# A fused transformer block on one core: column sums issued later, and a block compression with both halves of its weights side by side

## The chip, the cores and the metric

One core of a Trainium2 chip. The time is device microseconds of one execution of the program; the median of several runs is given. Engines are named as in the profile: PE (TensorE: matmuls; PEld its weight loads), DVE (VectorE), ACT (ScalarE), POOL (GpSimd), SP (SyncE, which here only issues DMAs).

## What is computed

Two transformer blocks in a row on 512 tokens of width 1024 in float32. The first block is attention of two kinds with a mixture of experts; the change doesn't touch it. The second has two layers, each a mixer and an MLP of width 4096:

```python
for layer in range(2):
    h = rms_norm(x, norm_mix_pre[layer])
    m = mixer_a(h, ...) if layer == 0 else mixer_c(h, ...)
    x = x + rms_norm(m, norm_mix_post[layer])
    h = rms_norm(x, norm_mlp_pre[layer])
    x = x + rms_norm(relu(h @ w1) ** 2 @ w2, norm_mlp_post[layer])
```

`mixer_c` compresses its keys and its values before it attends to them. From each of 31 windows of 32 tokens, which start 16 tokens apart, it makes one vector per group, for four groups of width 64:

```python
idx = 16 * arange(31)[:, None] + arange(32)[None, :]
def compress(z, pe, w1, w2):                  # w1: (32, 64, 64)
    blk = z[:, idx] + pe[:, None, :]
    hdn = gelu(einsum('bnlgd,lde->bnge', blk, w1))
    return hdn @ w2
```

## The kernel before

Activations lie transposed: 128 of the 1024 features on the partitions, tokens along the free dimension. Weights come by DMA on SP's queue as slabs of 128 x 1024 floats, and each is split into a high part (ACT, line 167) and a low part (DVE, line 168). A product is then three matmuls per block of 128 features: high by high (line 195), low by high (198), high by low (199). One such triple is called a step below; with 256 tokens a pass over 8 output chunks of 8 blocks is 64 steps.

The end of each mixer and of each MLP runs in halves of 256 tokens (`halves`). A first pass does chunk 0 for both halves and the other seven for the first half. A second pass does seven chunks, 56 steps, for the second half. While PE runs the second pass, the first half is finished by `post`, a Python generator that `weave` advances by one `yield` for each step of the pass. `post` for the second half is handed on and is woven into the opening pass of whatever follows, one `yield` for two steps: the first 64 steps of the MLP, or the opening of `mixer_c` (32 steps of chunks, then the values, where two steps count as one).

`post` does this: column sums of the squares of the mixer's output (`rstd`, with `col_sum` at line 325, a power on POOL, and `spread` matmuls), one `yield`; then for each of 8 blocks of features the normed output (DVE, line 1509), the new `x` (POOL, 1510), its high and low part for what follows (ACT 364, DVE 365), its square (ACT 281, the last one 290) and the running sum `acc` (DVE, 282), one `yield` each; then some empty yields; then `col_mean` of the new `x`, which is eight small matmuls with one moving column (line 325) and one DVE operation. `mlp_left` keeps the result in `mlp_eps`, which is read at the end of the MLP. `mix_left` makes `mix_rcol` (POOL, 1542) and `mix_rrow` (PE, 1547; ACT, 1549) of it, which the evacuations of `mixer_c` read. The empty yields are 12 ahead of an MLP and 4 ahead of `mixer_c`.

The order in the text is not the order on the engines. A planner deals the instructions out to the engines before the run: of those that it reckons ready at a time it takes the one that comes first in the text. What stands in an engine's queue is then fixed and runs in that order.

`compress` runs twice, for values and for keys. It loads its weights into a free part of `x` as 16 blocks of 128 x 64, each for two neighbouring tokens (`z` holds a copy of itself on partitions 64 to 127, one token further on). 16 products with 31 columns per group (line 1986) add up the 32 tokens of a window, 16 more with one column (line 1990) make the bias from `pe`. Each is two PE instructions in the trace. Then follow the bias (DVE), a gelu (DVE and ACT), and a product with `w2` (lines 2005 and 2014). Between its parts, `yield 1`, `yield 6` and `yield 3` let as many steps of the gates and projections through.

Of the kernel before, what the change touches and what calls it, by code (L numbers as in the profile page):

```python
# [9 lines left out]
F32 = mybir.dt.float32  # L10
# [4 lines left out]
OP = mybir.AluOpType  # L15
# [4 lines left out]
P = 128  # L20
S = 512
# [37 lines left out]
R1 = 0.4  # L59
R5 = 0.4  # L60
APP = 0

def run(steps):
    for _ in steps:
        pass


def weave(main, *fill):  # L70

    fill = chain(*fill)
    due = 0.0
    for n in main:
        due += n
        while due >= 1:
            next(fill, None)
            due -= 1
    run(fill)


class Net:
# [284 lines left out]
    def apply(self, x, g, r, hi, lo, bias=None):  # L367
# [5 lines left out]
        t = self.np.tile([P, 256], F32, name="ap_t", bufs=APB)  # L373
        if bias is None and APP:
            nc.gpsimd.tensor_mul(t, x, r)
# [1119 lines left out]
            self.nc.scalar.dma_start(x[:, k:k + 4], xr[:, k:k + 4])  # L1495
        return x

    def post(self, acc, g, tok, nxt, dump, save=False, left=None, eps=None):


        nc, m = self.nc, self.m
        r = self.rstd(acc, D, eps=eps)
        yield 1
        x = self.x
        acc = self.acc_tile("acc2")
        o = self.t["out"].rearrange("(k p) t -> p k t", p=P)
        for k in range(NC):
            t = self.np.tile([P, 256], F32, name="ap_t", bufs=APB)
            nc.vector.scalar_tensor_tensor(t, m[:, k, tok], g[:, k:k + 1], r, op0=OP.mult, op1=OP.mult)  # L1509
            nc.gpsimd.tensor_add(x[:, k, tok], x[:, k, tok], t)  # L1510
            if left is not None:
                self.raw_apply(x[:, k, tok], nxt[:, k:k + 1], self.h[0][:, k, tok], self.h[1][:, k, tok])
            if nxt is not None:
                self.sq_half(acc, x[:, k, tok], k, nc.vector if k >= PSQ else nc.gpsimd)
            elif k % 2:
                nc.sync.dma_start(o[:, k - 1:k + 1, tok], x[:, k - 1:k + 1, tok])
            yield 1
        self.dump(dump, x[:, :, tok], (slice(None), slice(None), tok))
        if nxt is not None:
            if save:  # L1520
                self.save_x(x, tok)
            if left is not None:
                for _ in range(12 if left == self.mlp_left else 4):
                    yield 1
                yield from left(self.col_mean(acc, D), tok)
                return
            r = self.rstd(acc, D)
            yield 1
            yield from self.apply_steps(x, nxt, r, tok)
# [22 lines left out]
    def halves(self, src, s0, rhs, g, nxt, dump, evac, save=False, left=None, eps=(None, None)):  # L1552

        accs, seen = [self.acc_tile("acc") for _ in range(2)], [0, 0]

        def e(i, ps, hb):
            tok = self.HALVES[hb]
            evac(i, ps, tok)
            self.sq_half(accs[hb], self.m[:, i, tok], seen[hb])
            seen[hb] += 1  # L1560

        out = [self.half_steps(src, s0, o, lambda hb: tuple(a[:, :, self.HALVES[hb]] for a in rhs), e, pool)
               for o, pool in zip(self.orders(NC, BOTH), ((), PL2))]
        tails = [self.post(accs[hb], g, tok, nxt, dump, save, left, eps[hb]) for hb, tok in enumerate(self.HALVES)]
        run(out[0])
        weave((RATE for _ in out[1]), tails[0])
        return tails[1]
# [407 lines left out]
    def compress(self, nm, z, tp, Kc, Vc):  # L1975
        nc, t = self.nc, self.t
        w1 = self.x[:, 4:6] if nm == "k" else self.x[:, 6:8]
        w1 = w1.rearrange("p k t -> p (k t)").rearrange("p (a e) -> p a e", a=16)
        w2 = tp.tile([64, 64], F32, name="cw2")
        nc.sync.dma_start(w1, t[f"cmp_w1_{nm}"].rearrange("(a p) e -> p a e", p=P))  # L1980
        nc.sync.dma_start(w2, t[f"cmp_w2_{nm}"])
        nc.gpsimd.memset(z[64:P, :, S - 1:], 0.0)
        ps = self.ptile()
        hv = ps[:64, :124].rearrange("p (g n) -> p g n", g=4)
        for a in range(16):
            nc.tensor.matmul(hv, w1[:, a], z[:, :, 2 * a:2 * a + 481:16], start=(a == 0), stop=(a == 15))
        pb = self.ptile()
        pe = self.v(f"pe_{nm}")
        for a in range(16):
            nc.tensor.matmul(pb[:64, :1], w1[:, a], pe[:, a:a + 1], start=(a == 0), stop=(a == 15))  # L1990
        yield 1
        bias = tp.tile([64, 1], F32, name="c_b")
        nc.vector.tensor_copy(bias, pb[:64, :1])
        x, u = tp.tile([64, 124], F32, name="c_x"), tp.tile([64, 124], F32, name="c_u")
        nc.vector.tensor_scalar(x, ps[:64, :124], bias, None, op0=OP.add)
        nc.vector.tensor_mul(u, x, x)
        nc.vector.tensor_scalar(u, u, 0.044715, 1.0, op0=OP.mult, op1=OP.add)
        nc.vector.tensor_mul(u, u, x)
        nc.scalar.activation(u, u, AF.Tanh, scale=0.7978845608028654)
        nc.vector.scalar_tensor_tensor(u, u, 1.0, x, op0=OP.add, op1=OP.mult)  # L2000
        nc.vector.tensor_scalar(u, u, 0.5, None, op0=OP.mult)
        yield 6
        ps = self.ptile()
        if nm == "k":
            nc.tensor.matmul(ps[:64, :124], w2, u, start=True, stop=True)
            src = ps[:64, :124].rearrange("p (g n) -> p g n", g=4)
            c = slice(32, 63)
            nc.scalar.copy(Kc["k1"][:64, :, c], src)
            nc.vector.tensor_sub(Kc["k2"][:64, :, c], src, Kc["k1"][:64, :, c])
            for d in (Kc["k1"][64:], Kc["k3"][:64]):  # L2010
                nc.vector.tensor_copy(d[:, :, c], Kc["k1"][:64, :, c])
        else:
            for g in range(4):
                nc.tensor.matmul(ps[:31, 64 * g:64 * g + 64], u[:, 31 * g:31 * g + 31], w2, start=True, stop=True)
            src = ps[:31, :256].rearrange("p (g d) -> p g d", g=4)
            for r in range(4):
                c = slice(64 * (r % 2), 64 * (r % 2) + 64)
                nc.scalar.copy(Vc[0][32 * r:32 * r + 31, :, c], src)
                if r < 2:
                    nc.vector.tensor_sub(Vc[1][32 * r:32 * r + 31, :, c], src, Vc[0][32 * r:32 * r + 31, :, c])  # L2020
        yield 3
# [264 lines left out]
```

## Time and profile before

| | |
|---|---|
| median of 3 runs | 2320.84 us (2317.47 to 2324.62) |
| the profiled execution | 2322.31 us |
| its span, first to last instruction | 2320.6 us |
| mean granted TensorE clock | 0.969 |
| PE busy | 2191.8 us (94%) |
| PEld busy | 1828.6 us (79%) |
| DVE busy | 1392.3 us (60%) |
| ACT busy | 1110.4 us (48%) |
| POOL busy | 419.1 us (18%) |

All from one profiled execution, but for the first row. A busy PE is not a PE at its peak, since its matmuls overlap and its clock has two levels; how fast it goes is read from the distance of the starts of like matmuls. A granted clock of 1.00 is 2.4 GHz, 0.50 is 1.2 GHz.

### The profile page before, as it was taken

The page shows a single profiled execution, that of the slowest core. Times are in us where ns is not written, and L with a number is a line of the kernel's source. Part 1 is how long each engine was busy: PE and PEld are TensorE (multiplying, and loading weights), DVE is VectorE, ACT ScalarE, POOL GpSimd, SP SyncE. Part 2 cuts the span into 40 slices and gives each one's busy share as a digit, 9 for nine tenths or more (in the row PEclk, how much of TensorE's full clock was granted, in tenths as well). Part 3 has the DMA queues.
Part 4 walks back from the last instruction along what each step waited for, and adds up shares of the span by engine and source line. Part 5 has one row for each costly group of instructions (what it writes and reads, how often), then busy time and mean ns, then how long its engine had stood idle before and what let it go on. Part 6 is the DMA issues. An engine that isn't in the chain of part 4 may idle for free. (4 is left out here: it accounts for less than half of the span.)

```text
span 2320.6 us, 32117 instructions
## 1 busy us (share of the span) xinstructions
PE 2191.8 (94%) x12260; PEld 1828.6 (79%) x12260; DVE 1392.3 (60%) x1994; ACT 1110.4 (48%) x1854; POOL 419.1 (18%) x470
## 2 busy tenths in 40 slices
PE   5999999979999999999899999999999998999996
PEld 4778778967888797678898888987666688888886
DVE  7676765569999856664533344564777745343443
ACT  3554542448888764445543223352565635432231
POOL 4101000221111151101300000350234332000004
PEclk9999999979999989999899999999999998999998
DMA  6563264469999631124132222342122141322221
GB/s 238 148 190 109 82 218 164 174 231 357 356 354 354 226 140 49 63 72 169 65 118 92 100 100 92 100 132 59 45 69 61 44 154 61 126 96 100 96 77 37
DMA packets 127124, 320.10 MB, mean 138 GB/s; under 512 B 24720, under 2 KB 30096, under 8 KB 126963
## 3 DMA queue, kind: packets, MB, share of 16 engines
q1 hardware_dynamic: 111902, 286.56, 35.3%
q0 software_dynamic: 11200, 22.91, 4.1%
q10 hardware_dynamic: 3860, 8.51, 1.0%
q8 instruction: 98, 1.61, 0.3%
q14 instruction: 64, 0.52, 0.1%
HBM read 296.31 MB, written 18.69 MB: 136 GB/s over the span
## 5 line engine op out<-in xcount | busy, mean ns | idle before, releaser
L195 PE MATMUL acc<-h_hi,w_hi 128*128 128x512 f32 (+1 forms) x1464 | 520.1, 356 | 3.7 <-DVE q L428 1.7
L199 PE MATMUL acc<-h_hi,w_lo 128*128 128x512 f32 (+1 forms) x1464 | 513.5, 351 | 1.3 <-DVE w_lo L168 1.2
L198 PE MATMUL acc<-h_lo,w_hi 128*128 128x512 f32 (+1 forms) x1464 | 513.2, 351 | 0.0
L168 DVE TENSOR_TENSOR w_lo<-x_raw,w_hi 128x1024 fp32r<-128x1024 f32 x260 | 317.9, 1231 | 208.0 <-ACT w_hi L167 203.7
L167 ACT CAST w_hi<-x_raw 128x1024 fp32r<-128x1024 f32 x260 | 271.2, 1047 | 290.8 <-PE acc L198 246.0
L195 PEld LDWEIGHTS acc<-h_hi,w_hi 128*128 128x128 f32 x1464 | 284.1, 194 | 37.0 <-issue 2.7
L199 PEld LDWEIGHTS acc<-h_hi,w_lo 128*128 128x128 f32 x1464 | 283.6, 194 | 36.0 <-DVE w_lo L168 2.8
L198 PEld LDWEIGHTS acc<-h_lo,w_hi 128*128 128x128 f32 x1464 | 283.9, 194 | 29.9 <-issue 0.8
L168 DVE TENSOR_TENSOR w_lo<-w_raw,w_hi 128x1024 fp32r<-128x1024 f32 (+2 forms) x141 | 166.8, 1184 | 149.0 <-ACT w_hi L167 145.0
L167 ACT CAST w_hi<-w_raw 128x1024 fp32r<-128x1024 f32 (+2 forms) x141 | 143.6, 1019 | 223.9 <-PE acc L198 197.9
L195 PE MATMUL acc<-act_hi,w_hi 128*128 128x512 f32 (+1 forms) x640 | 222.7, 348 | 0.0
L198 PE MATMUL acc<-act_lo,w_hi 128*128 128x512 f32 (+1 forms) x640 | 222.5, 348 | 0.0
L199 PE MATMUL acc<-act_hi,w_lo 128*128 128x512 f32 (+1 forms) x640 | 222.4, 348 | 0.0
L282 POOL TENSOR_TENSOR acc<-acc,sq 128x256 f32<-128x256 f32 x60 | 54.7, 911 | 744.4 <-ACT sq L281 743.4
L195 PEld LDWEIGHTS acc<-act_hi,w_hi 128*128 128x128 f32 x640 | 121.7, 190 | 15.3 <-ACT act_hi L1610 0.3
L199 PEld LDWEIGHTS acc<-act_hi,w_lo 128*128 128x128 f32 x640 | 121.7, 190 | 15.0
L198 PEld LDWEIGHTS acc<-act_lo,w_hi 128*128 128x128 f32 x640 | 121.6, 190 | 15.0
L505 DVE TENSOR_TENSOR pl<-pexp,ph 128x512 fp32r<-128x512 f32 x144 | 116.9, 824 | 24.8 <-ACT ph L504 23.0
L1615 DVE TENSOR_TENSOR m<-m,acc 128x512 f32<-128x512 f32 (+1 forms) x64 | 35.2, 552 | 137.1 <-PE acc L199 137.1
L469 DVE TENSOR_REDUCE mx<-acc 128x1 f32<-128x128 f32 x192 | 89.0, 484 | 38.8 <-PE acc L468 37.1
L503 ACT ACTIVATE pexp<-sT 128x512 f32<-128x512 f32 x144 | 82.3, 572 | 32.6 <-PE sT L494 14.0
L195 PE MATMUL gu<-w_hi,xh 128*128 128x512 f32 x240 | 95.3, 397 | 0.0
(587 smaller groups left out, 4452.8 us busy)
## 6 DMA issues: line engine op xcount, KB each, us to landing
x_raw<-mlp_w SPq DMA_DIRECT2D x90, 512.0 KB
w_raw<-mlp_w SPq DMA_DIRECT2D x48, 512.0 KB
x_raw<-w_down SPq DMA_DIRECT2D x40, 512.0 KB
x_raw<-w_up SPq DMA_DIRECT2D x39, 512.0 KB
x_raw<-w_gate SPq DMA_DIRECT2D x38, 512.0 KB
w_raw<-w_in SPq DMA_DIRECT2D x20, 512.0 KB
h_raw<-w_up SPq DMA_DIRECT2D x19, 512.0 KB
h_raw<-w_gate SPq DMA_DIRECT2D x18, 512.0 KB
```

What stands on the lines that cost most here:

```text
L167: nc.scalar.copy(hi[:, :n], raw[:, :n])
L168: (eng or nc.vector).tensor_sub(lo[:, :n], raw[:, :n], hi[:, :n])
L195: mm(ps, l[0], r[0], start=start, stop=False)
L198: mm(ps, l[0], r[1], start=False, stop=False)
L199: return mm(ps, l[1], r[0], start=False, stop=stop).ins
L282: (eng or nc.gpsimd).tensor_add(acc[:, a:a + 256], acc[:, a:a + 256], sq)
L469: self.last_max = nc.vector.reduce_max(mx[:, c0 + qb:c0 + qb + 1], ps[:, :n], axis=AX.X).ins
L503: nc.scalar.activation(e[:, :o], ps[:, :o], AF.Exp)
L505: nc.vector.tensor_sub(pt[1][:, :o], e[:, :o], pt[0][:, :o])
L1615: nc.vector.tensor_add(self.m[:, i, tok], self.m[:, i, tok], ps)
```

## The change

The empty yields become a table. Ahead of an MLP they are 40 for the first half and 22 for the second, where both were 12; ahead of `mixer_c` they are 34 and 10, where both were 4. The last MLP has no `col_mean` and so none.

In `compress` the 32 tokens of a window are taken as two halves of 16. The weights of both halves lie side by side as 8 blocks of 128 x 128, loaded by two DMAs instead of one. 8 products with 32 blocks of 16 tokens per group give the first half's part on partitions 0 to 63 and the second's on 64 to 127; 8 more with two columns of `pe` give the bias in two parts, into the same PSUM tile. ACT copies the second half's part to partitions 0 to 63, DVE adds the bias parts, and one DVE operation adds the first half's part of block n, the bias, and the second half's part of block n + 1. The clearing of the last column of `z` on POOL goes.

```diff
--- before.py
+++ after.py
@@ -59,6 +59,7 @@
 R1 = 0.4
 R5 = 0.4
 APP = 0
+LATE = ((40, 22), (34, 10))
 
 
 
@@ -1495,7 +1496,8 @@
             self.nc.scalar.dma_start(x[:, k:k + 4], xr[:, k:k + 4])
         return x
 
-    def post(self, acc, g, tok, nxt, dump, save=False, left=None, eps=None):
+    def post(self, acc, g, tok, nxt, dump, save=False, left=None, eps=None, late=0):
+
 
 
         nc, m = self.nc, self.m
@@ -1520,7 +1522,7 @@
             if save:
                 self.save_x(x, tok)
             if left is not None:
-                for _ in range(12 if left == self.mlp_left else 4):
+                for _ in range(late):
                     yield 1
                 yield from left(self.col_mean(acc, D), tok)
                 return
@@ -1561,7 +1563,8 @@
 
         out = [self.half_steps(src, s0, o, lambda hb: tuple(a[:, :, self.HALVES[hb]] for a in rhs), e, pool)
                for o, pool in zip(self.orders(NC, BOTH), ((), PL2))]
-        tails = [self.post(accs[hb], g, tok, nxt, dump, save, left, eps[hb]) for hb, tok in enumerate(self.HALVES)]
+        tails = [self.post(accs[hb], g, tok, nxt, dump, save, left, eps[hb], LATE[save][hb])
+                 for hb, tok in enumerate(self.HALVES)]
         run(out[0])
         weave((RATE for _ in out[1]), tails[0])
         return tails[1]
@@ -1975,24 +1978,28 @@
     def compress(self, nm, z, tp, Kc, Vc):
         nc, t = self.nc, self.t
         w1 = self.x[:, 4:6] if nm == "k" else self.x[:, 6:8]
-        w1 = w1.rearrange("p k t -> p (k t)").rearrange("p (a e) -> p a e", a=16)
+        w1 = w1.rearrange("p k t -> p (k t)").rearrange("p (a h e) -> p a h e", a=8, h=2)
         w2 = tp.tile([64, 64], F32, name="cw2")
-        nc.sync.dma_start(w1, t[f"cmp_w1_{nm}"].rearrange("(a p) e -> p a e", p=P))
+        src = t[f"cmp_w1_{nm}"].rearrange("(h a p) e -> h p a e", p=P, h=2)
+        for h in range(2):
+            nc.sync.dma_start(w1[:, :, h], src[h])
         nc.sync.dma_start(w2, t[f"cmp_w2_{nm}"])
-        nc.gpsimd.memset(z[64:P, :, S - 1:], 0.0)
+
         ps = self.ptile()
-        hv = ps[:64, :124].rearrange("p (g n) -> p g n", g=4)
-        for a in range(16):
-            nc.tensor.matmul(hv, w1[:, a], z[:, :, 2 * a:2 * a + 481:16], start=(a == 0), stop=(a == 15))
-        pb = self.ptile()
+        hv = ps[:, :P].rearrange("p (g n) -> p g n", g=4)
+        w1 = w1.rearrange("p a h e -> p a (h e)")
         pe = self.v(f"pe_{nm}")
-        for a in range(16):
-            nc.tensor.matmul(pb[:64, :1], w1[:, a], pe[:, a:a + 1], start=(a == 0), stop=(a == 15))
+        for a in range(8):
+            nc.tensor.matmul(hv, w1[:, a], z[:, :, 2 * a:2 * a + 497:16], start=(a == 0), stop=(a == 7))
+        for a in range(8):
+            nc.tensor.matmul(ps[:, P:P + 2], w1[:, a], pe[:, a:a + 9:8], start=(a == 0), stop=(a == 7))
         yield 1
-        bias = tp.tile([64, 1], F32, name="c_b")
-        nc.vector.tensor_copy(bias, pb[:64, :1])
-        x, u = tp.tile([64, 124], F32, name="c_x"), tp.tile([64, 124], F32, name="c_u")
-        nc.vector.tensor_scalar(x, ps[:64, :124], bias, None, op0=OP.add)
+        bias, h2 = tp.tile([64, 1], F32, name="c_b"), tp.tile([64, P + 2], F32, name="c_u")
+        nc.scalar.copy(h2, ps[64:P, :P + 2])
+        nc.vector.tensor_add(bias, ps[:64, P:P + 1], h2[:, P + 1:])
+        x, u = tp.tile([64, 124], F32, name="c_x"), h2[:, :124]
+        nc.vector.scalar_tensor_tensor(x.rearrange("p (g n) -> p g n", g=4), hv[:64, :, :31], bias,
+                                       h2[:, :P].rearrange("p (g n) -> p g n", g=4)[:, :, 1:], op0=OP.add, op1=OP.add)
         nc.vector.tensor_mul(u, x, x)
         nc.vector.tensor_scalar(u, u, 0.044715, 1.0, op0=OP.mult, op1=OP.add)
         nc.vector.tensor_mul(u, u, x)
```

## Rows read from the trace of the kernel before

**Rows 1.** The page, part 1: busy us, share of the span, instructions.

```profile
PE 2191.8 (94%) x12260; PEld 1828.6 (79%) x12260; DVE 1392.3 (60%) x1994; ACT 1110.4 (48%) x1854; POOL 419.1 (18%) x470
```

**Rows 2.** Waits of PE: who <- whom, us in total, times, longest.

```profile
PE csum L325 <- DVE acc L282: 22.5, 6, 4.5
```

**Rows 3.** PE's timeline at four waits: start, us; in brackets the idle time.

```profile
1116.21 0.24 PE L325 MATMUL csum<-ones,acc 128*128 128x1 f32 x1 [4.50 <-DVE acc L282]
...
1151.18 0.34 PE L325 MATMUL csum<-ones,acc 128*128 128x1 f32 x1 [3.60 <-DVE acc L282]
...
1494.13 0.34 PE L325 MATMUL csum<-ones,acc 128*128 128x1 f32 x1 [3.89 <-DVE acc L282]
...
1526.48 0.34 PE L325 MATMUL csum<-ones,acc 128*128 128x1 f32 x1 [2.41 <-DVE acc L282]
```

**Rows 4.** Line 195 (one a step) from pass start to wait; PE count first.

```profile
1097.90:1111.70 13.80, 9.21 (x32) 6.03 (x32) 1.00 0.11 38
1128.75:1147.50 18.75, 13.39 (x48) 8.99 (x47) 1.00 0.48 170
1473.15:1490.20 17.05, 11.94 (x42) 7.86 (x41) 1.00 0.19 63
1503.15:1524.00 20.85, 13.46 (x47) 8.76 (x46) 1.00 0.22 77
```

**Rows 5.** PE's timeline, like matmuls ahead of the first wait and behind it.

```profile
1110.83 0.28 PE L195 MATMUL acc<-h_hi,w_hi 128*128 128x256 f32 x1
1110.95 0.28 PE L198 MATMUL acc<-h_lo,w_hi 128*128 128x256 f32 x1
...
1119.44 0.41 PE L195 MATMUL acc<-h_hi,w_hi 128*128 128x256 f32 x1
1119.65 0.41 PE L198 MATMUL acc<-h_lo,w_hi 128*128 128x256 f32 x1
```

**Rows 6.** Stretches behind waits: us, busy PE, PEld, DVE, ACT, POOL; granted clock.

```profile
1116.83:1123.66 6.83, 6.83 (x34) 6.83 (x33) 0.32 (x2) 1.42 (x4) 2.00 (x3) 0.50 0.01 2
...
1150.96:1161.20 10.24, 10.02 (x47) 10.05 (x48) 2.70 (x9) 3.33 (x9) 1.18 (x1) 0.50 0.01 2
...
1492.30:1499.12 6.82, 4.99 (x23) 4.95 (x24) 3.70 (x7) 3.30 (x9) 3.34 (x5) 0.50 0.79 246
...
1918.96:1925.79 6.83, 5.37 (x25) 5.40 (x26) 2.03 (x6) 2.53 (x7) 2.88 (x4) 0.50 0.00 0
...
1956.51:1963.33 6.82, 6.54 (x31) 6.25 (x30) 1.29 (x5) 2.56 (x7) 0.00 (x0) 0.50 0.00 0
```

**Rows 7.** ACT's timeline: the last square of x in the second wait.

```profile
1153.30 0.40 ACT L290 ACTIVATE sq<-x 128x256 f32<-128x256 f32 x1
```

**Rows 8.** The stretch ahead of the second wait, columns as in rows 6.

```profile
1128.75:1147.50 18.75, 18.75 (x156) 18.40 (x154) 14.61 (x24) 12.37 (x29) 6.60 (x7) 1.00 0.48 170
```

**Rows 9.** PE's timeline, the first compression and its product with w2.

```profile
1558.53 6.94 PE L1986 MATMUL acc<-m,x 128*64 128x124 f32 x32
1565.29 1.99 PE L1990 MATMUL acc<-vec,x 128*64 128x1 f32 x32
1567.21 0.54 PE L195 MATMUL acc<-h_hi,w_hi 128*48 128x512 f32 x1
...
1573.74 0.63 PE L2014 MATMUL acc<-cw,c_u 64*31 64x64 f32 x8
```

**Rows 10.** Column sums without a wait: us, busy PE and PEld, clock.

```profile
1099.10:1099.75 0.65, 0.65 (x6) 0.65 (x6) 1.00 0.00 0
```

**Rows 11.** DVE's timeline, the end of the first gelu.

```profile
1569.40 0.22 DVE L2001 TENSOR_SCALAR c_u<-c_u 64x124 f32<-64x124 f32 x1
```

**Rows 12.** Waits of SP, 1500 to 1600 us: us in total, times, longest.

```profile
SPq L1981 <- PE acc L2014: 21.7, 1, 21.7
```

**Rows 13.** 1600 to 1880 us: PE's waits; DMA issues, median us to landing.

```profile
PE acc L467 <- DMA q<-q: 3.1, 3, 1.9
...
q<-q POOLq DMA_DIRECT2D x7, 256.0 KB, 5.2
```

## Prediction

> **What bounds the kernel now.** The page comes first: TensorE is busy 2191.8 of 2320.6 us, so in most stretches the time is the length of PE's own queue, and time can only be won where PE stands idle, runs at its lower clock, or does work that can be left out [rows 1]. The view of who waited for whom, for PE alone, is read next. Its largest entry is a wait of a column sum (`csum`, line 325) for the running sum of squares (`acc`, line 282): 22.5 us in 6 waits, the longest 4.5 [rows 2]. The timeline shows where they are: 4.50 us at 1116.21 and 3.60 at 1151.18 (the first `out_proj` and the first MLP's opening pass), 3.89 at 1494.13 and 2.41 at 1526.48 (end of that MLP, start of `mixer_c`) [rows 3]. The other two, in the second `out_proj` and the second MLP, are what is left: 22.5 - 4.50 - 3.60 - 3.89 - 2.41 = 8.1 us. PE takes its queue in order, so every one of these waits holds back matmuls whose operands are ready.
>
> Then the same stretches with the granted clock. Behind each wait PE runs at the lower of its two levels (0.50, which is 1.2 of 2.4 GHz): it is busy 6.83 us in 1116.83 to 1123.66, 10.02 us in 1150.96 to 1161.20, 5.37 and 6.54 us behind the two waits of the second `out_proj`, and 4.99 us behind the wait at 1494 [rows 6]. What that costs is read from the distance between starts of 256-column matmuls: 1110.83 to 1110.95, 0.12 us, at full clock; 1119.44 to 1119.65, 0.21 us, at the low one [rows 5]. Of a low-clock stretch 1 - 0.12/0.21 = 0.43 is lost.
>
> **The column sums, place by place.** `post` is a side thread that is advanced one `yield` at a time while a pass of matmuls runs. The change only adds empty yields ahead of `col_mean`. Where that puts the eight column-sum matmuls I count in steps of the pass (one step is three matmuls, 3 x 0.12 = 0.36 us). In the first `out_proj` the old text puts them behind 1 + 8 + 12 = 21 yields, so into step 22; in the trace 32 steps ran between the start of that pass and the stall [rows 4]. So the planner that orders the engines held them back by ten steps on its own reckoning of when `acc` is ready, and was still 4.50 us, 12.5 steps, too early. A new place counts only if it is later than the one the planner chose: new place = the later of text and planner.
>
> First half of each `out_proj`: the new text is 1 + 8 + 40 = 49 yields, step 50 of 56. PE is needed to be past step 32 + 12.5 = 44.5 for the sum to be ready. 50 is behind that by 5.5 steps, 2.0 us, so the 4.50 us go. Second half (the MLP's opening pass, one yield in two steps): old text step 44, found at 48 by the count that includes both edges [rows 4]; needed 3.60 / 0.36 = 10 steps more, 58. New text 2 x 32 = step 64, the last of the pass. The last square (ACT) starts at 1153.30 and takes 0.40 [rows 7]; PE, which stopped near 1147.58 (1151.18 - 3.60), would get to step 64 some 16 to 17 steps later, at 1153.4 to 1153.7. I take this as no wait, with 0.5 us as its upper bound. The second layer has the same structure. Idle time won: 4.50 + 3.60 + 8.1 = 16.2 us.
>
> With the waits the low clock behind them should go, as no other stop of that size stands in front of these four stretches: (6.83 + 10.02 + 5.37 + 6.54) x 0.43 = 28.8 x 0.43 = 12.4 us. The lower bound is 0, if the clock falls there anyway. (The Trainium skill, TensorE: Matmul & The Clock Gate, Terms, prices a throttled time at 1 - K/N, here one half, so 14.4 us for the same time; the rows give 0.43, since the full-clock distance of 0.12 us is not half of 0.21. The row is used.)
>
> In `mixer_c` the story differs. First half: old text step 14, found at step 42 [rows 4]; needed 3.89 / 0.36 = 10.8 more, about 53. The new text is 1 + 8 + 34 = 43 yields, step 44. That is later than the planner's 42 by only two steps. Second half: old text step 28, found after 47 k-steps [rows 4]; the new text is step 40, which is 48 k-steps (32 of the chunks, then two to a step). So one. I book 2 x 0.36 + 0.36 = 1.1 us and let the rest of these waits stand. Upper bound: both waits and the low clock of 1492.30 to 1499.12 go, 3.89 + 2.41 + 4.99 x 0.43 = 8.4 us. Lower bound: 0. I take 1.1, since the counts are rows and a later reckoning by the planner is not.
>
> What moves with the sums: behind them come a 128x2 operation on DVE (nobody waits for `mlp_eps` until the MLP's end) and, in `mixer_c`, the power on POOL, the `spread` matmuls and `mix_rrow`; POOL has `nsa_setup` queued behind the power. They move by the same one to two steps, under 1 us, which I book at nothing: until then PE has matmuls of the pass in its queue, and where the pass runs out the next one follows; without that cover it would be their length, under 1 us in each half.
>
> **What is late next.** With PE no longer stopped, ACT and DVE must deliver the split weights at the full rate. In the stretch ahead of the second stall, PE is busy 18.75 of 18.75 us, DVE 14.61 and ACT 12.37 [rows 8], with the split in it; both have room. I book nothing, and up to 2 us in each of four places for the range.
>
> **The compression.** Now: 32 matmul instructions of 124 columns from 1558.53 to 1565.29, 6.76 us, 0.211 each, then 32 of one column to 1567.21, 1.92 us [rows 9]. That is 8.7 us per pass, PE without a gap. After: 16 of 128 columns and 16 of two, with 128 weight columns instead of 64. The moving operand keeps its step of 16 tokens, so I scale by columns: 0.211 x 128/124 = 0.218, 16 x 0.218 = 3.49 us. The bias matmuls are too short to be set by two columns; the nearest row is the column sum, one column against 128 weight columns: six in 0.65 us, 0.108 each [rows 10], so 16 x 0.108 = 1.73 us. Halving their number therefore wins almost nothing. New pass 5.2, won 3.5, in two passes 6.9 us. All of it is PE time with PE busy on both sides, so it counts in full.
>
> The lower bound for this term: if the wider weight load doesn't hide under the matmul, 16 x 0.108 = 1.7 us more per pass, 3.5 in all, leaving 3.4. (The Trainium skill, TensorE: Matmul & The Clock Gate, Part 3, The mechanism, says that a weight load overlaps running matmuls only if its row group differs, which it doesn't here; by that the sum would be 3.5 us smaller. The trace speaks against it: 256-column matmuls with 128 weight columns start every 0.12 us [rows 5], while a load of that width alone takes 0.108 [rows 10].)
>
> Behind the matmuls the chain gets one ACT copy out of PSUM and one small DVE addition longer, and loses a copy. It ended at 1569.40 + 0.22 = 1569.62; PE came for it at 1573.74 [rows 9, 11]. Those 4.1 us are steps of the gate projection, which stay; the two operations cost well under 1 us, so nothing. If that cover were gone, their length would be PE's wait, twice. The two cleared columns on POOL go: nobody waited. On SP each 512 KB weight load becomes two of half the size, one issue more each; SP waited 21.7 us behind `cw2` for the first compression to end [rows 12], with PE not starved, so a second issue costs nothing there.
>
> **Sum.** 16.2 + 12.4 + 1.1 + 6.9 = 36.6 us. The profiled execution took 2322.31 us around its span of 2320.6, and the runs' median is 2320.84, so the profile is 1.5 us above the median. From the median: 2284 us.
>
> **Rivals.** (a) The planner puts the `mixer_c` sums late enough too, because its reckoning shifts with the rest: 8.4 instead of 1.1, 2277 us. Against it: the counts above. (b) The idle time goes and the clock falls nonetheless, or ACT and DVE fall behind by a similar amount: 12.4 us come back, 2297 us. For it: in the stall at 1151 the tail's last additions were DVE's, which has little left over in such a pass; against it: no stop of PE is left ahead of those stretches. (c) The change doesn't do what it says: the planner keeps the sums about where they are, since the text was not what set their place; only the compression counts, 2314 us. Against it: a planner can't easily put an instruction ahead of matmuls that the text has earlier and that are ready. (d) Slower: the order of all engines from 1558 on is dealt anew, and the DMA copies of q (POOL queue, 256 KB, 5.2 us to landing) come onto PE's path in each of the eight head pairs, where now PE waits 3.1 us for them in three waits [rows 13]. Eight waits of 5.2 us, each with the low clock that followed a wait of 4.50 (6.83 x 0.43 = 2.9), less the 3.1: 62 us, so 2346. It decides from 36.6 / 8 = 4.6 us a pair. Against it: the compression's instructions stand before all pairs and only get shorter.
>
> **Chances.** Forecast 0.55, (a) 0.13, (b) 0.20, (c) 0.08, (d) 0.04. Range 2270 to 2303: it takes in (a), the forecast and (b), with 6 to 7 us on either side for the bounds of the compression (3.5) and of the split weights; left out are (c) and (d), and the far ends. A measurement of this kernel can tell about 0.3%, 7 us: faster means under 2314, which (c) just misses or meets. Faster 0.92, same 0.06, slower 0.02.
>
> **What would show it.** In the profile after, PE's waits for `acc` of line 282 should have four entries fewer and two of about 3 and 2 us left, near the start of `mixer_c`. The low clock behind 1116, 1151, 1919 and 1957 should be gone: a low clock there without a wait says (b). The compression should show 16 matmuls of 128 columns at 0.218 us and 16 short ones at 0.108; 0.33 for the former says that loads aren't hidden. If column sums sit at their old step counts, it is (c). Waits for copies of q beyond 10 us say (d). The forecast is wrong if the second halves' sums, now last in their pass, wait for the final square by more than 0.5 us each.

## The result and the profile after

The changed kernel takes 2288.77 us (median of four runs, 2284.09 to 2293.03) where the kernel before takes 2322.73 beside it: 34.0 us less, ratio 0.9854 with an interval of 0.9822 to 0.9885. The forecast was 2284, 36.6 us less, and a range of 2270 to 2303. The profiled execution after has a span of 2291.3 us, 29.3 under that of before. Timed a second time, in the run `after_again` below, the ratio was 0.9872 (0.9850 to 0.9894).

The page's line of busy times, part 1, answers to [rows 1]: PE has 64 instructions and 16.0 us of work less, and idles 13.3 us less.

```profile
PE 2175.8 (95%) x12196; PEld 1816.5 (79%) x12196; DVE 1388.9 (61%) x1994; ACT 1109.7 (48%) x1856; POOL 422.4 (18%) x468
```

The waits of PE, the view of [rows 2] and [rows 13] (who waited for whom: us in total, times, longest). Lines of the code have moved down by one, so line 325 of before is 326 here, and 282 is 283.

```profile
PE csum L326 <- DVE acc L283: 5.1, 2, 3.1
...
PE acc L468 <- DMA q<-q: 2.5, 3, 1.6
...
PE csum L326 <- POOL acc L283: 1.2, 2, 0.6
...
PE spread L1549 <- POOL mix_rcol L1544: 0.7, 1, 0.7
```

The first entry was 22.5 us in 6. Four waits are gone and two are left, of the size that was booked. The third and the fourth are new and small: the next column sum in the same pass, that of the other half, waits for POOL once in each layer, and the spread of `mixer_c` waits for the power on POOL once. The copies of q cost 2.5 us where they cost 3.1.

PE's timeline at the places of [rows 3] (start, us; idle time in brackets): the first two rows are the first `out_proj`, then the MLP's opening pass, `mixer_c` twice, and the second layer's two.

```profile
1119.96 0.28 PE L326 MATMUL csum<-ones,acc 128*128 128x1 f32 x2
1124.48 0.38 PE L326 MATMUL csum<-ones,acc 128*128 128x1 f32 x2 [0.61 <-POOL acc L283]
...
1148.56 0.28 PE L326 MATMUL csum<-ones,acc 128*128 128x1 f32 x2
...
1480.86 0.35 PE L326 MATMUL csum<-ones,acc 128*128 128x1 f32 x2 [3.08 <-DVE acc L283]
...
1514.79 0.35 PE L326 MATMUL csum<-ones,acc 128*128 128x1 f32 x2 [2.05 <-DVE acc L283]
...
1906.55 0.28 PE L326 MATMUL csum<-ones,acc 128*128 128x1 f32 x2
...
1935.20 0.28 PE L326 MATMUL csum<-ones,acc 128*128 128x1 f32 x2
```

The same stretches by window (us, then busy time of PE, PEld, DVE, ACT and POOL, granted clock, DMA share, GB/s), against [rows 6] and [rows 8]:

```profile
1097.00:1127.00 30.00, 28.93 (x241) 28.51 (x240) 16.07 (x29) 16.02 (x37) 13.60 (x16) 1.00 0.06 20
1127.00:1150.00 23.00, 23.00 (x193) 22.77 (x192) 18.46 (x33) 16.88 (x42) 9.24 (x9) 1.00 0.41 137
1481.31:1491.55 10.24, 9.58 (x45) 9.28 (x45) 1.75 (x4) 2.04 (x5) 5.39 (x6) 0.50 0.52 170
1515.45:1522.27 6.82, 6.82 (x35) 6.82 (x34) 4.08 (x8) 3.56 (x8) 2.93 (x8) 0.50 0.94 290
1900.00:1935.00 35.00, 34.37 (x285) 33.91 (x285) 24.83 (x44) 23.68 (x56) 16.37 (x18) 1.00 0.27 91
```

At `out_proj` and the MLP the clock is 1.00 throughout, and PE is busy 23.00 of 23.00 us with DVE at 18.46 and ACT at 16.88: neither is late. In `mixer_c`, behind the two waits that were left, the low clock lasts 10.24 and 6.83 us; before it lasted 6.82 us behind the first [rows 6] and 3.41 behind the second (from 1526.42).

The compression, PE's timeline, against [rows 9]: 16 instructions of 128 columns from 1547.93 to 1551.40, 0.217 each, then 16 of two columns to the next matmul at 1553.24, 0.115 each. That is 5.3 us where 8.7 were.

```profile
1547.93 3.65 PE L1993 MATMUL acc<-m,x 128*128 128x128 f32 x16
1551.40 1.98 PE L1995 MATMUL acc<-vec,x 128*128 128x2 f32 x16
1553.24 0.64 PE L196 MATMUL acc<-h_hi,w_hi 128*48 128x512 f32 x1
```

**Where the time went, stretch by stretch.** The DVE operation that writes `w_lo` runs 464 times, in the same order in every kernel here. The start of one such operation, less the start of the same one in the profile of before, says how far a kernel is ahead at that point; the difference between two points is what it won (negative) in the stretch between them. The seven points stand at 1075, 1170, 1492, 1554, 1599, 1888 and 1972 us of the profile of before. "Sums 1" is the first `out_proj` with the MLP's opening pass, "sums 2" the second layer's. The stretch from 1170 to 1492 is left out: it moved by 0.04 us at most in every kernel; so is the tail behind 1972.

| kernel | to 1075, untouched | sums 1 | mixer_c | compression | pairs, untouched | sums 2 |
|---|---|---|---|---|---|---|
| before_again | +0.92 | -2.31 | -0.58 | +0.06 | +0.50 | -0.17 |
| the changed kernel | +1.93 | -15.23 | +2.75 | -7.26 | +2.08 | -13.49 |
| after_again | +2.22 | -15.22 | -1.40 | -7.25 | +2.12 | -13.50 |
| late_only | -1.28 | -15.21 | +1.37 | +0.03 | +3.79 | -13.49 |
| cmp_only | -1.61 | -1.98 | -1.02 | -7.24 | -1.69 | +2.19 |
| mix_old | -0.98 | -15.22 | -0.91 | -7.26 | +1.20 | -13.50 |
| mix_44_13 | -2.35 | -15.21 | +1.80 | -7.27 | -2.35 | -13.52 |
| mix_dve | +1.85 | -15.22 | -0.25 | -8.81 | +1.46 | -13.50 |
| fill | +2.47 | -7.50 | +0.39 | +0.02 | +1.88 | -5.79 |
| first28 | -1.36 | -11.93 | +1.20 | -7.23 | +1.68 | -10.30 |
| first20 | +5.22 | -7.66 | +1.15 | -7.24 | +2.29 | -6.58 |
| cmp_inter | +1.38 | -15.21 | -1.67 | -8.87 | -0.11 | -14.06 |
| both2 | -2.17 | -15.22 | -0.91 | -9.11 | -0.33 | -13.49 |

Read the columns. Where the table has its full effect, eight profiles give 15.2 us at sums 1 to a few hundredths, and seven of them 13.5 at sums 2; the new compression as written gives 7.25 in seven of eight profiles. In mixer_c two executions of one kernel differ by 4 us, and the untouched stretches spread over 6 to 8 us.

### The profile page after: what moved, and what is told of

It is laid out like the page before. It is cut to its first block, busy times and chain, and to the rows that moved or that the text cites. A ratio compares the mean times of both kernels' runs of the same rounds, so it can differ in the third digit from the quotient of the medians.

```text
span 2291.3 us, 31977 instructions
## 1 busy us (share of the span) xinstructions
PE 2175.8 (95%) x12196; PEld 1816.5 (79%) x12196; DVE 1388.9 (61%) x1994; ACT 1109.7 (48%) x1856; POOL 422.4 (18%) x468
## 3 DMA queue, kind: packets, MB, share of 16 engines
q1 hardware_dynamic: 111934, 286.56, 36.6%
q8 instruction: 98, 1.61, 0.3%
## 4 chain that ended last, share of the span: by engine, by line
PE 46%; DVE 4%; POOL 2%; DMA 2%; issue 2%; ACT 2%; SPq 0%; ACTq 0%; POOLq 0%; DVEq 0%
PE acc L196 13%; PE acc L199 13%; PE acc L200 13%; PE pv L518 2%; PE sT L495 2%; PE acc L468 1%; DVE pl L506 1%; DMA rb<-coef_dram 1%; DMA q<-q 1%; POOL x L1512 1%; DVE ap_t L1511 1%; POOL acc L283 1%; POOL wb L2110 1%; DVE w_lo L169 0%; DVE h_lo L366 0%
## 5 line engine op out<-in xcount | busy, mean ns | idle before, releaser
L196 PEld LDWEIGHTS acc<-act_hi,w_hi 128*128 128x128 f32 x640 | 122.9, 192 | 15.2 <-ACT act_hi L1613 0.3
```

Of the source, the lines that this page charges most:

```text
L196: mm(ps, l[0], r[0], start=start, stop=False)
```

## The experiments

**One half of the change at a time.** `late_only` is the kernel before with the table, `cmp_only` the changed kernel with the old counts.

```diff
# late_only, on the kernel before
+LATE = ((40, 22), (34, 10))
...
-                for _ in range(12 if left == self.mlp_left else 4):
+                for _ in range(late):
...
# cmp_only, on the changed kernel
-LATE = ((40, 22), (34, 10))
+LATE = ((12, 12), (4, 4))
```

> The kernel before with the table of late yields alone; the compression is left as it was. Theory (terms 16.2 idle, 12.4 clock, 1.1 mixer_c; compression's 6.9 gone from the sum): 29.7 us under the kernel before, ratio about 0.987; the four waits of out_proj and the MLP gone, the low clock behind them gone, two waits of about 3 and 2 us left at the start of mixer_c. Rival 1 (the gain is mostly the compression's, because it deals the order of the second layer anew): under 20 us won, and waits of about 8 us stay in the second layer. Rival 2 (the clock falls nonetheless): 17 us won.

> The changed kernel with the table set back to 12, 12 and 4, 4, so that only the new compression stands. Theory: 16 long matmuls at 0.218 and 16 short at 0.108 in each pass, 5.2 us where 8.7 were; 6.9 us won, ratio 0.997, and PE's wait for the running sums as before at 22.5 us in 6. Rival (the shorter pass uncovers the chain of the gelu behind it, or the lower clock there lasts longer): 0 to 3 us won, with a wait of PE in front of the second matmul of the compression.

`late_only` has a ratio of 0.9907 (0.9888 to 0.9927), 21.6 us less; `cmp_only` 0.9969 (0.9951 to 0.9987), 7.2 us less. The second is what was expected, with the waits of before in place:

```profile
PE csum L326 <- DVE acc L283: 22.5, 6, 4.5
```

The first falls 8 us short of 29.7 in its timing, beyond its interval, while its trace has 15.21 + 13.49 - 1.37 = 27.3 us at the three places, with no low clock at either pair of sums and no wait there but the two of 0.6 us for POOL. What its profile lacks beside that lies among the pairs, which no edit touches (+3.79 us). Both rivals of `late_only` fall: no wait of 8 us stays in the second layer, and the clock doesn't fall nonetheless. The halves don't depend on each other: 28.7 us at the sums is the same with the new compression and without.

**Idle time and clock apart.** Here the sums stay near their early place, but PE has work while it would wait. (They stand 29 steps behind the `spread` in front of them in the first halves, where it was 28, and 35 in the second halves, where it was 30.)

```diff
# fill, on the kernel before
-                for _ in range(12 if left == self.mlp_left else 4):
+                for _ in range((23, 16)[tok.start // 256] if left == self.mlp_left else 4):
                     yield 1
+                if left == self.mlp_left:
+                    self.fill(tok)
...
+    def fill(self, tok):
+        self.dummy = self.pn.tile([P, S], F32, name="csum", tag=self.ntags[0])
+        h = self.h[0]
+        for i in range(35 if tok.start == 0 else 28):
+            self.nc.tensor.matmul(self.dummy[:, :256], h[:, 0, tok.start:tok.start + P], h[:, 0, tok], start=True, stop=True)
```

> The kernel before, with 35 products of 128x256 that nobody reads put in front of the column sums of the first half of each out_proj and 28 in front of those of the second half, at the old places but for one or two steps. At 0.12 us each they are 4.2 and 3.4 us of work where PE stood idle 4.5 and 3.6 us; the useful work and its place stay as they are. Theory (the clock falls because PE stood idle): nothing of the 16.2 us of idle time is won, the low clock behind the four places is gone, so 12.4 us under the kernel before, ratio 0.995. Rival (the clock falls there whatever PE did before, because of the short column sums or of what follows): 0 us, low clock behind all four places as before.

The ratio is 0.9954 (0.9937 to 0.9972), as the theory had it. PE's timeline and the four places by window (columns as above):

```profile
1114.38 4.36 PE L1537 MATMUL csum<-h_hi 128*128 128x256 f32 x35
1118.80 0.38 PE L325 MATMUL csum<-ones,acc 128*128 128x1 f32 x2
```

```profile
1110.00:1127.00 17.00, 17.00 (x143) 16.86 (x143) 8.70 (x19) 8.78 (x23) 8.02 (x10) 1.00 0.09 32
1140.00:1165.00 25.00, 24.55 (x204) 24.32 (x203) 14.58 (x31) 15.60 (x40) 6.33 (x6) 1.00 0.11 36
1895.00:1920.00 25.00, 24.53 (x204) 24.17 (x203) 13.65 (x26) 11.41 (x29) 11.73 (x14) 1.00 0.06 22
1930.00:1960.00 30.00, 29.57 (x244) 29.09 (x244) 18.52 (x36) 18.96 (x47) 9.30 (x9) 1.00 0.25 88
```

The idle time that is left is 0.45 and 0.42 us for the last square, in the second halves, and the 0.47 us of a `spread` that waits as before; the clock is 1.00 at all four places. Useless work, put where PE stood idle, made the kernel 7.50 + 5.79 = 13.3 us shorter at those places. So the clock fell at these places because PE stood idle, and not because of the short sums, which are there as before. This is the clock term by itself, 12.4 forecast, but for some 0.4 us: the useless work and the waits left take 16.9 us, the waits before took 16.5.

**How much lateness is needed.** The changed kernel's table with a smaller first entry:

```diff
# first28
+LATE = ((28, 22), (34, 10))
# first20
+LATE = ((20, 22), (34, 10))
```

> The changed kernel with 28 in place of 40 for the first half ahead of an MLP; nothing else differs. The sums stand 6 steps behind their place of before and 12 ahead of that in the changed kernel. Theory: a wait of 4.50 - 6 x 0.36 = 2.3 us is left in each first half, and the low clock follows it as it followed the longer wait (6.83 x 0.43 = 2.9): 2 x 5.2 = 10.4 us over the changed kernel, ratio to the kernel before about 0.991. Rival (a wait of half the length leaves the clock alone): 4.6 us over it.

> The changed kernel with 20 in place of 40 for the first half ahead of an MLP, which by the text is step 30 of the pass: behind the old text's step 22, ahead of the step 32 where the kernel before had the sums. Theory (the place is the later of the text's and the planner's): they stay at step 32 and PE waits 4.5 us in both first halves, with about 6.8 us of low clock behind it: 2 x (4.5 + 2.9) = 14.8 us over the changed kernel, ratio to the kernel before about 0.992. Rival (8 yields more move them by 8 steps): a wait of 4.5 - 2.9 = 1.6 us.

PE's timeline of `first28`, then of `first20`:

```profile
1114.89 0.35 PE L326 MATMUL csum<-ones,acc 128*128 128x1 f32 x2 [2.38 <-DVE acc L283]
...
1902.83 0.35 PE L326 MATMUL csum<-ones,acc 128*128 128x1 f32 x2 [2.37 <-DVE acc L283]
```

```profile
1121.43 0.56 PE L326 MATMUL csum<-ones,acc 128*128 128x1 f32 x2 [4.50 <-DVE acc L283]
...
1914.20 0.35 PE L326 MATMUL csum<-ones,acc 128*128 128x1 f32 x2 [4.51 <-DVE acc L283]
```

With 20 yields the text is eight steps later than before and the wait is 4.50 us, exactly as before: the sums haven't moved. The timelines show it directly: between the `spread` in front and these sums stand 28 steps in the kernel before, 28 in `first20`, 34 in `first28` and 46 in the changed kernel, the same in both layers. That is the rule "the later of text and planner". It costs 7.57 + 6.92 = 14.5 us against the changed kernel (14.8 expected; ratio 0.9939, 0.9914 to 0.9964). With 28 yields six steps count, and the wait is 2.38 (2.3 expected from 6 x 0.36). The clock, though, falls for 3.41 us and not for 6.83, by the windows of `first28` (us, PE's busy time, granted clock, DMA share, GB/s):

```profile
1115.52:1118.93 3.41, 3.41 (x17) 0.50 0.03 7
1904.00:1907.41 3.41, 3.41 (x18) 0.50 0.00 0
```

So it costs 3.30 + 3.19 = 6.5 us against the changed kernel: more than the waits alone (4.8), less than the 10.4 of the theory; the ratio is 0.9891 (0.9865 to 0.9917). It adds up: 4.75 of waits and 2 x 3.41 x 0.43 of clock, less the 1.2 us of POOL waits, which this kernel hasn't. Both sides were half right: a wait of 2.4 us still takes the clock down, but for half as long.

**mixer_c.** Its entry set back, and then raised to where the sums should find their operands ready:

```diff
# mix_old
+LATE = ((40, 22), (4, 4))
# mix_44_13
+LATE = ((40, 22), (44, 13))
# mix_dve: as mix_44_13, and in halves():
-            self.sq_half(accs[hb], self.m[:, i, tok], seen[hb])
+            self.sq_half(accs[hb], self.m[:, i, tok], seen[hb], self.nc.vector if save and hb else None)
```

> The changed kernel with the mixer_c entry of the table set back to 4, 4; nothing else differs. Theory: the three steps that mixer_c's sums moved are worth 1.1 us, so this is 1 us slower than the changed kernel, ratio to the kernel before 0.986, with waits of 3.9 and 2.4 us there again. Rival (moving the sums by a step or two lengthened the low clock behind them, 10.24 and 6.83 us against 6.83 and 3.41, which costs 6.8 x 0.43 = 2.9): this is about 2 us faster than the changed kernel and its low-clock stretches there are 6.83 and 3.41 again.

> The changed kernel with the mixer_c entry raised from 34, 10 to 44, 13. That puts the two sums 10 and 12 steps (3.6 and 4.3 us) further behind than in the changed kernel, where the waits left are 3.08 and 2.05 us. Theory (an idle PE and the low clock behind it go together): 3.08 + 2.05 idle and (10.24 + 6.83) x 0.43 = 7.3 us of low clock go, 12 us under the changed kernel, ratio to the kernel before about 0.980. Rival (the wait only changes its name, because the row of scales that hangs on the sums is wanted by the evacuations of the next pass): PE waits as long for PSUM space or for the spread row, 0 to 3 us won.

`mix_old`: 0.9874 (0.9853 to 0.9894), with waits of 3.89 and 2.42 us again; not to be told from the changed kernel. `mix_44_13`: 0.9864 (0.9841 to 0.9886), nothing like the 12 us expected. Both waits for `acc` are gone, and in their place stand two others. The first is for the spread, with this queue on POOL (timeline of `mix_44_13`):

```profile
1477.08 1.81 POOL L283 TENSOR_TENSOR acc<-acc,sq 128x256 f32<-128x256 f32 x1 [1.67 <-ACT sq L282]
...
1483.16 0.72 POOL L283 TENSOR_TENSOR acc<-acc,sq 128x256 f32<-128x256 f32 x1 [0.53 <-ACT sq L282]
1483.84 0.71 POOL L1544 TENSOR_TENSOR mix_rcol<-rs_c,mh 128x2 f32<-128x2 f32 x1
```

```profile
1484.61 1.22 PE L1549 MATMUL spread<-idf,mix_rcol 128*128 128x128 f32 x4 [5.89 <-POOL mix_rcol L1544]
```

The power that the spread needs stands on POOL behind five running sums of the other half, the last four 1.25 us apart because each waits for a square from ACT. The second is 2.33 us long: where PE stood idle for the later sum, it now waits for a split weight (`w_lo`). In the view of waits this line reads 1.6, 2, 0.9 for the changed kernel, and here:

```profile
PE acc L199 <- DVE w_lo L169: 3.1, 2, 2.3
```

The rival of that run was right: the waits only changed their names.

> The kernel of the run with 44 and 13 for mixer_c, and the running sums of squares of m in the second half ahead of mixer_c made by DVE (0.41 us each) instead of POOL (0.71). In that run PE waited 5.89 us for a spread whose power stood on POOL behind five of these sums, and 13.65 us of low clock lay around it. Theory (POOL's queue held it back): the wait falls under 1 us and the low clock to 3.4: 5.9 + 10.2 x 0.43 = 10.3 us under that run, ratio to the kernel before about 0.982. Rival (what holds it back are ACT's squares, which come late on either engine, or DVE now delays the split weights): under 4 us won, with waits of PE for split weights or for the next column sum.

0.9854 (0.9830 to 0.9878), against 0.9864 without the edit: within the interval, not the 10 us of the theory. PE still waits 3.89 us for the same spread, and 2.33 us for a split weight as in `mix_44_13`. DVE and ACT, timeline of `mix_dve`:

```profile
1484.31 0.43 DVE L283 TENSOR_TENSOR acc<-acc,sq 128x256 f32<-128x256 f32 x1 [0.48 <-ACT sq L282]
1485.22 0.43 DVE L283 TENSOR_TENSOR acc<-acc,sq 128x256 f32<-128x256 f32 x1 [0.48 <-ACT sq L282]
1485.56 0.15 DVE L337 TENSOR_SCALAR rs_c<-csum 128x2 f32<-128x2 f32 x1
```

```profile
1482.86 0.42 ACT L282 ACTIVATE sq<-m 128x256 f32<-128x256 f32 x1 [1.78 <-DVE acc L283]
1483.86 0.42 ACT L282 ACTIVATE sq<-m 128x256 f32<-128x256 f32 x1 [0.58 <-DVE acc L283]
```

Now the mean (`rs_c`), which comes ahead of the power, stands on DVE behind the same chain. A square waits for an addition and an addition for its square, whichever engine adds; what stands behind that chain in the adding engine's queue is late. By the program the squares have two buffers, which an addition frees. No run gave them more, so whether more buffers would shorten the chain stays open. The rival held here too.

**The compression's order.** The bias products in turn with the long ones, into another PSUM tile; `both2` does so with the tile taken from the column sums' pool (in `cmp_inter` the planner kept only the first pass in turn) and has mixer_c's entry back at 4, 4.

```diff
# cmp_inter (both2: pb = self.pn.tile([P, S], F32, name="spread", tag=self.ntags[1]))
+        pb = self.ptile()
         for a in range(8):
             nc.tensor.matmul(hv, w1[:, a], z[:, :, 2 * a:2 * a + 497:16], start=(a == 0), stop=(a == 7))
-        for a in range(8):
-            nc.tensor.matmul(ps[:, P:P + 2], w1[:, a], pe[:, a:a + 9:8], start=(a == 0), stop=(a == 7))
+            nc.tensor.matmul(pb[:, :2], w1[:, a], pe[:, a:a + 9:8], start=(a == 0), stop=(a == 7))
...
```

> The changed kernel with the 8 bias products of the compression taken in turn with its 8 long ones, into a PSUM tile of their own, in place of one run of short ones at the end; one ACT copy of two columns more. Theory (the run of short products is what the 3.41 us of low clock behind each compression follows): the same 5.2 us of products, and the low clock gone: 2 x 3.41 x 0.43 = 2.9 us under the changed kernel. Rival (the low clock there belongs to the long products with their 128 columns, or to what is in front of them): no difference, 3.41 us of low clock at either pass.

> The changed kernel with two edits: the mixer_c entry of the table back at 4, 4, and the bias products of the compression in turn with the long ones in both passes, into a tile of the column sums' pool. Theory: the low clock behind either compression goes (2 x 3.41 x 0.43 = 2.9 us) and what mixer_c gave back is kept (1 to 3 us), so 4 to 6 us under the changed kernel, ratio to the kernel before 0.984. Rival (the clock's low stretches move elsewhere, or the products in turn take longer): within 2 us of the changed kernel.

> The changed kernel once more, beside the two that follow, so that they can be compared on one chip. Theory: 28 us at the two out_proj and MLP places, 7 in the compression, 1 to 3 us given back in mixer_c, so 32 us under the kernel before, ratio 0.986; the clock's phases in the untouched first block move a single profile by some 4 us either way. Rival (34 us as forecast without the loss in mixer_c): ratio 0.985 or less.

`cmp_inter` is at 0.9862 (0.9840 to 0.9884), `both2` at 0.9873 (0.9848 to 0.9899), the changed kernel beside it at 0.9872 (theory 0.986; 0.985, its rival's bound, is the end of its interval): no difference that can be timed, and the 0.984 expected of `both2` lies outside its interval. In the traces the compression wins 8.87 and 9.11 instead of 7.25 us; but so it does in `mix_dve`, 8.81, where the order is the old one and one pass has no low clock behind it. PE doesn't wait at the compression, yet in the profiles with the new one a low clock of 3.41 us follows 16 of the 17 passes with the bias products in a run of their own, and 1 of the 3 with the products in turn; the one is in `both2`, whose window reads

```profile
1545.48:1548.89 3.41, 3.41 (x10) 0.50 0.00 0
```

So the run of short products isn't all of the cause; with three passes that stays open. `after_again` shows another point: with the same code as the changed kernel its low clock in mixer_c is 6.83 us, not 17, and it wins 1.40 us there where the first profile lost 2.75. So that loss wasn't the code's alone.

**Before, once more.**

> The kernel before once more, for a second profile. In the profiles of the changed kernel and its variants the two stretches that no edit touches (up to 1075 us, and 1599 to 1888 us of the kernel before) stand -2.4 to +5.2 and -2.4 to +3.8 us from the first profile of before. Theory (that is chance in the low clock there): ratio 1.000, and this profile moves by as much in the same two stretches, while the four places of the sums and the compression stay within 0.5 us of the first profile except for the length of their low clock. Rival (the changed kernels lose a microsecond or two there for good): the two stretches are as in the first profile to within 0.5 us.

The ratio is 0.9995 (0.9976 to 1.0015). The untouched stretches move by 0.92 and 0.50, less than in most others, so neither the theory (as much) nor the rival (within 0.5) holds in both. Where before has its waits, it moves too: the low clock at the four places is 10.24, 3.41, 6.83 and 6.83 us in all, in `cmp_only` (same waits) 6.83, 6.83, 10.24 and 10.24. The windows of `before_again`, then of `cmp_only` (us, PE's busy time, granted clock, DMA share, GB/s):

```profile
1115.19:1125.43 10.24, 8.30 (x39) 0.50 0.01 2
1152.73:1156.15 3.42, 3.39 (x16) 0.50 0.00 0
1917.32:1924.15 6.83, 5.15 (x24) 0.50 0.00 0
1954.87:1961.69 6.82, 6.64 (x32) 0.50 0.00 0
```

```profile
1112.71:1119.54 6.83, 4.94 (x23) 0.50 0.01 2
1150.26:1157.09 6.83, 6.73 (x32) 0.50 0.01 2
1904.61:1914.85 10.24, 7.96 (x37) 0.50 0.00 0
1942.15:1952.39 10.24, 10.01 (x47) 0.50 0.01 2
```

The same wait is followed by a low clock of another length in another execution. In `before_again` that is nearly all of the 2.31 us at sums 1: PE is busy 11.7 us at the low clock there, 16.9 in the first profile, and 0.43 of the difference is 2.2. At sums 1 and 2 three profiles of that code stand 0, -2.31, -1.98 and 0, -0.17, +2.19 us apart.

## Why the prediction was right

**The sums ahead of the MLP: 28.6 forecast (16.2 idle, 12.4 clock), 28.7 measured (15.2 at sums 1, 13.5 at sums 2).** The steps held one by one. The planner's floor held: a text of step 30 left the sums where they were (`first20`). The count of steps held: six steps took 2.12 of 4.50 us (`first28`), 18 took it all. The second halves' sums, last in their pass, find the last square ready: they start at 1148.56 without a wait, and so the 0.5 us kept as an upper bound weren't needed. Two waits of 0.6 us for POOL are new and weren't booked; the clock made up for them (28.7 - 16.2 + 1.2 = 13.7 us for the clock, 13.3 by `fill`, 12.4 booked). The booking by rows, 0.43 of the low-clock time, is a little under both. The chance in the low clock's length can be taken out: PE is busy 28.8, 23.5 and 29.6 us at the low clock at the four places in `before`, `before_again` and `cmp_only`, and `fill` is 13.3, 10.8 and 13.5 us ahead of them there, 0.46 of it each time (0.47 to 0.48 with the 0.4 us named at `fill`). Half of it, 14.4 by the rule of the Trainium skill (TensorE: Matmul & The Clock Gate, Terms), is a little over. So the mechanism was right; that the POOL waits and the price of the clock, both off by about 1 us, cancel to 0.1 us is luck. Rival (b) is out: at these places there was no low clock without idle time.

**The compression: 6.9 forecast, 7.25 measured.** 0.217 for the long ones (0.218 booked) and 0.115 for the short ones (0.108). In the two passes the products went from 17.5 to 10.6 us, 6.9 won as booked; the other 0.3 us lies beside them. The lower bound, loads not hidden, would have shown 0.33; the wider load is hidden.

**mixer_c: 1.1 forecast; the waits shrank by 0.81 and 0.36 us, 1.17 in all, and 0.66 came back.** The count of steps (two and one) was right to a tenth of a us. The term that was missed is the power on POOL behind the running sums, for which the spread now waits 0.66 us (0.92 in `after_again`). The prediction named that power among what moves and covered it with "under 1 us". The upper bound of this term, 8.4 us if the sums were late enough (rival (a)), was wrong, even without the 3.41 us of low clock behind the second wait that it left out: `mix_44_13` and `mix_dve` put them there and won nothing that can be timed, since the chain of squares and a split weight take the waits' place. On balance mixer_c's stretch is between -1.67 and +2.75 us in six executions with the new counts and between -1.02 and +0.39 in six with the old ones; the two can't be told apart there. The low clock in that stretch is 13.7 to 17.1 us in four of the six with the new counts and 6.8 in two, against 6.8 to 10.2 with the old ones: that later sums lengthen it, the rival of `mix_old`, is neither shown nor out.

**The sum: 36.6 forecast, 34.0 and (by the second timing, 0.0128 x 2320.93) 29.7 measured.** The places add up to 28.7 + 7.25 = 36.0 us, mixer_c about nothing. Between that and the timings 2 to 6 us are missing. Part is chance: the profile of before isn't the middle of its kind at the sums (the three above are 0.8 us ahead of it on the mean, -1.43 + 0.67), and the untouched stretches of the changed kernel's profile lie 4.0 us behind (1.93 + 2.08). Whether a microsecond of that is there for good isn't settled: among the pairs eight of the twelve profiles of other kernels are behind the first of before, the twelve by 1.0 us on the mean, and `before_again` is behind by 0.50. It isn't the low clock alone: with 0.43 of PE's busy time in it taken off, the twelve are still 0.6 to 2.3 us behind and `before_again` 0.7. Rival (c) and rival (d) are out: the sums moved, and waits for q cost 2.5 us against 3.1.

## To carry to other kernels

Where a planner orders the engines, a delay in the text does nothing until it passes the planner's own place; so count, in steps of the matmul pass, both where an instruction stands and where its operand is ready, and delay it by the difference. A short wait of TensorE can cost more than its length, here 13 us lost to the slow clock beside 16 us of waiting, and even useless matmuls in the gap win that part back. Before a late instruction is moved to where its operand is ready, look at the queues of what comes behind it: in mixer_c the next step stood behind the same chain, and the wait only moved on.

## What the hardware showed that was not expected

- The low clock behind one and the same wait isn't of one length: behind the 3.60 us wait of the MLP's opening pass it was 10.24 us in the first profile of before, 6.83 in `cmp_only` and 3.41 in `before_again`. Behind a wait of 2.38 us it was 3.41. Behind the second wait of mixer_c, 2.05 to 2.42 us, it was 6.83 in the first profile of the changed kernel, and there was none in `after_again`, `mix_old`, `cmp_inter` and `both2`.
- That chance alone moves two executions of one kernel by 4 us in a stretch of 62 (mixer_c, +2.75 and -1.40), more than any edit to mixer_c was found to bring. Two single profiles are to be compared stretch by stretch, and not by their spans.
